# Attention logits: each head on its own 64 rows of the matmul array, instead of zero-padded keys on all 128

## The chip, the core and the metric

The kernel runs on one core of one Trainium2 chip. The metric is the device time of one execution in microseconds (us). The engines of the core run side by side, each with its own list of instructions in fixed order, and wait for one another through semaphores: PE (TensorE, matmuls), DVE (VectorE), ACT (ScalarE), POOL (GpSimd) and SP (the queue that issues DMAs). PE has two kinds of instruction, which the profile lists apart: a weight load (PEld), which puts the stationary operand into the array, and the matmul (PE), which streams the moving operand past it into a bank of PSUM. There are eight such banks here, each of 512 fp32 columns on 128 partitions.

## The reference

Two layers on x (1024 tokens, 1024 channels): dilated sliding-window attention, then a state-space layer. The change is in the attention, whose core is

```
DILATED_GROUPS = ((128, 1), (512, 4), (2048, 16))       # 3 groups, 16 heads of 64 channels
proj = h @ w_in                                         # q, k, v of each group, and a gate z
for g, (window, dilation):                              # token t looks at t - j*dilation, j = 0..window/dilation
    logits = einsum(q, k) * 64**-0.5 + rel_bias[bucket(distance)]
    lse = logsumexp(logits);  p = exp(logits - lse);  o = einsum(p, v)
o = sum over g of softmax_g(lse) * o_g
x = x + rms_norm((o * silu(z)) @ w_out)
...                                                     # layer 2: state-space, gelu, gated, projected
```

All arithmetic is fp32-like. The kernel gets this from fp32r matmuls by splitting each operand into a rounded part and a rest (`hi`, `lo`), and adding three products: hi*hi, hi*lo, lo*hi.

## The kernel before

The work runs in stages on one core: the values of all heads (0 to 372 us of the profiled execution), attention (372 to 1145 us), the output projection and norm of layer 1, then layer 2. In attention, `attn_pair` takes a pair of heads p = 0..7 (2 x 64 channels = 128 partitions), and in it the three groups g = 0, 1, 2. For each group it

- loads and splits the weights of q and k (`load_w`: DMA, ACT rounds to `whi`, POOL makes the rest `wlo`),
- projects (`proj_half`: 24 matmuls of 128x512 into a bank of the pool `psj`, twice for q, twice for k),
- brings the result from PSUM to SBUF, scaled, reordered and split (`evac_q`, `evac_k`: ACT writes hi, DVE writes lo),
- and calls `attn_unit` for u = 0, 1, four query tiles of 128 queries each: logits on PE into a bank of the pool `psl`, bias and maximum on DVE (line 488, one instruction per head and query tile, 128 or 256 keys wide), exponential on ACT, then transposes (`pt`, line 510) and the products with the values (`pso`, line 559 or 585).

Each of the four PSUM pools `psj`, `psl`, `pst`, `pso` has two banks.

How the two heads of a pair are kept apart in the logits: every matmul uses all 128 rows of the array, and a contraction has only 64 channels. For g = 0 and 1 the other 64 rows carry a second product. `qh` holds hi of head 0 on rows 0-63 and lo of head 0 on rows 64-127; `ql` holds the same of head 1, halves exchanged. `kh[:, h]` holds hi of head h on both halves (a second copy, line 214), and `kl[:, h]` holds lo of head h on one half and zeros on the other. So `q x kh` gives two of the three products and `q x kl` the third: two matmuls per head, four per query tile, 128 or 256 columns each. For g = 2 (128 keys per query tile) `qh` and `ql` hold both heads, and `kh[:, h]`, `kl[:, h]` have zeros on the rows of the other head, so that one matmul of 2 x 128 columns serves both heads: three per query tile. `zero_other` (POOL, line 221) writes those zeros into `kh` before each g = 2. There is one buffer of `kh` and one of `kl`, so the keys of a group are written only after the logits of the one before.

A scheduler sets the order on each engine, from the dependencies and its own estimate of times; work in `high_priority` (the weight loads and the evacuations of q and k) is pulled ahead. It mixes the logits of one group with the projections of the next, which is what the order below shows.

Of the kernel before, what the change touches and what calls it, by code (L numbers as in the profile page):

```python
# [23 lines left out]
P = 128  # L24
S = 1024
D = 1024
KT = 8
H = 512
# [8 lines left out]
ORD = (1, 4, 8)  # L37
# [3 lines left out]
def f32(ap):  # L41
    return ap.bitcast(F32)
# [3 lines left out]
HEADS = (slice(0, 64), slice(64, 128))  # L46
# [32 lines left out]
def split(c, hi, lo, src, scale=None, engine=None):  # L79

    nc = c.nc
    if scale is None:
        nc.scalar.copy(hi, src)  # L83
        return (engine or nc.vector).tensor_tensor(lo, src, f32(hi), op=ALU.subtract)  # L84
    else:
        nc.scalar.activation(hi, src, AF.Copy, scale=scale)
        nc.vector.scalar_tensor_tensor(lo, src, scale, f32(hi), op0=ALU.mult, op1=ALU.subtract)
# [101 lines left out]

def evac_q(c, ps, g, t0, q):  # L190


    nc = c.nc
    n = ps.shape[1] // ORD[g]
    at = (S - t0) // ORD[g] - n
    sv = ps.rearrange("p (l r) -> p r l", r=ORD[g])[:, :, ::-1]
    q = [t.rearrange("p (r l) -> p r l", r=ORD[g])[:, :, at:at + n] for t in q]
    a, b = HEADS
    for dh, dl, src in (((q[0], q[1], sv),) if g == 2 else ((q[0][a], q[0][b], sv[a]), (q[1][b], q[1][a], sv[b]))):
        nc.scalar.activation(dh, src, AF.Copy, scale=0.125)  # L200
        nc.vector.scalar_tensor_tensor(dl, src, 0.125, f32(dh), op0=ALU.mult, op1=ALU.subtract)


def evac_k(c, ps, g, t0, kh, kl):


    n = ps.shape[1] // ORD[g]
    at = t0 // ORD[g]
    sv = ps.rearrange("p (l r) -> p r l", r=ORD[g])
    for s in range(2):  # L210
        dh, dl = (t[:, s, :].rearrange("p (r l) -> p r l", r=ORD[g])[:, :, at:at + n] for t in (kh, kl))
        split(c, dh[HEADS[s]], dl[HEADS[s]], sv[HEADS[s]])
        if g < 2:
            c.nc.scalar.copy(dh[HEADS[1 - s]], sv[HEADS[s]])  # L214


def zero_other(c, t):

    for s in range(2):
        rows = HEADS[1 - s]  # L220
        c.nc.gpsimd.tensor_copy(t[rows, s, :], c.zt[rows].to_broadcast([64, S]))


def load_first(c, a, k):
# [35 lines left out]
class Quads:  # L260
# [45 lines left out]
    done, jobs = 0, {}  # L306
# [151 lines left out]
def ms_col(g, n, h, qt):  # L458

    return (n * 16 + h * 8 + 7 - qt, n * 16 + h * 8 + (qt ^ 1), n * 16 + h * 8 + qt)[g]  # L460


def attn_unit(c, g, u, q, k, v, bt, ms, O):


    nc = c.nc
    qh, ql = q
    kh, kl = k
    lg = c.attn.tile([P, 2, 4, 256], F32, tag="lg", name="lg", bufs=3)
    tiles = []  # L470
    for j in range(4):
        qt = u * 4 + j
        m = (7 - qt, 1 - qt % 2, 0)[g]
        start = (max(m - 1, 0) * P, qt // 2 * 256, qt * P)[g]
        w = 256 if m else 128
        tiles.append(w)
        ps = c.psl.tile([P, 2, 256], F32, tag="psl", name="psl")
        qs = slice(qt * P, qt * P + P)
        ks = slice(start, start + w)
        if g == 2:  # L480
            jobs = [(ps[:, :, 0:w], a, b[:, :, ks]) for a, b in ((qh, kh), (qh, kl), (ql, kh))]
        else:
            jobs = [(ps[:, h, 0:w], (qh, ql)[h], b[:, h, ks]) for h in range(2) for b in (kh, kl)]
        for n, (o, a, b) in enumerate(jobs):
            nc.tensor.matmul(o, a[:, qs], b, start=n == 0, stop=n == len(jobs) - 1, skip_group_check=True)  # L485
        for h in range(2):
            col = ms_col(g, 0, h, qt)
            nc.vector.tensor_tensor_reduce(  # L488
                lg[:, h, j, 0:w], ps[:, h, 0:w], bt[:, h, 256 - w:256], scale=1.0, scalar=-3.0e38,
                op0=ALU.add, op1=ALU.max, accum_out=ms[:, col:col + 1])  # L490
    nm = c.small.tile([P, 2, 4], F32, tag="nm", name="nm")
    at = (4 - 4 * u, 4 * u, 4 * u)[g]
    mx = ms[:, 0:16].rearrange("p (h t) -> p h t", h=2)[:, :, at:at + 4]
    nc.vector.tensor_scalar(nm, mx, -1.0, None, op0=ALU.mult)  # L494
    for h in range(2):
        for j, w in enumerate(tiles):
            col = ms_col(g, 1, h, u * 4 + j)
            b = (3 - j, j ^ 1, j)[g]
            nc.scalar.activation(lg[:, h, j, 0:w], lg[:, h, j, 0:w], AF.Exp, bias=nm[:, h, b:b + 1],  # L499
                                 accum_out=ms[:, col:col + 1])  # L500
    (pv_last if g == 2 else pv_first)(c, g, u, lg, v, O)
    if u == 1:
        put_ms(c, g, ms)
# [148 lines left out]
def attn_pair(c, p, w_in, h):  # L652
    nc = c.nc
    c.pair = p
    O = []
    for g in range(3):
        qh = c.attn.tile([P, S], F32R, tag="qh", name="qh", bufs=2)
        ql = c.attn.tile([P, S], F32R, tag="ql", name="ql", bufs=2)
        w = load_w(c, w_in[g * 8 + p])
        for th in range(2):  # L660
            src = proj_half(c, w, h[th])
            with c.tc.high_priority(AHEAD):
                evac_q(c, src, g, th * H, (qh, ql))
        bt = load_bias(c, p, g)
        if g == 2:
            zero_other(c, c.kh)
        w = load_w(c, w_in[(3 + g) * 8 + p])
        for th in range(2):
            src = proj_half(c, w, h[th])
            with c.tc.high_priority(AHEAD):  # L670
                evac_k(c, src, g, th * H, c.kh, c.kl)
        v = load_v(c, p, g)
        rotations(c, p, g)
        if g == 1:
            run_merge(c)
        ms = c.small.tile([P, 32], F32, tag="ms", name="ms")
        for u in range(2):
            attn_unit(c, g, u, (qh, ql), (c.kh, c.kl), v, bt, ms, O)
            if p and g == u == 0:
                merge_weights(c, p - 1)  # L680
    if p == 7:
        merge_weights(c, p)
    c.merge = lambda: merge(c, p, O)


def run_merge(c):
    if c.merge:
        c.merge()
    c.merge = None
# [20 lines left out]
def attention(c, a):  # L710
    nc, tc = c.nc, c.tc
    c.h = h = []
    c.w_engine = nc.vector
    c.merge = c.compact = None
    for th in range(2):
        hh = c.pa.tile([P, KT, H], F32R, tag=f"a{th}", name=f"hh{th}")
        hl = c.pa.tile([P, KT, H], F32R, tag=f"a{2 + th}", name=f"hl{th}")
        h.append((hh, hl))
    with tc.tile_pool(name="vphase", bufs=1, side="right", reuse_waits="tile") as pool:
        c.vslot = lambda n, dt: pool.tile([P, 4, H], dt, tag=f"v{n}", name=f"v{n}")  # L720
        c.vextra = pool.tile([P, 256], F32, tag="extra", name="extra")
# [12 lines left out]
        nc.sync.dma_start(gain, bass.AP(src.tensor, src.offset, [[0, P], [1, D]]))  # L734
        nc.vector.tensor_copy(c.identr, ident)

        def rows(i):
            if i + 1 < 8:
                load_x(i + 1)
            norm_transpose0(c, xs[i], sq, gain, h[i // 4], slice(i % 4 * P, i % 4 * P + P))  # L740

        v_phase(c, a, rows)

    c.attn = c.es_attn.enter_context(tc.tile_pool(name="attn", bufs=1, side="right", reuse_waits="tile"))
    c.kh = c.attn.tile([P, 2, S], F32R, tag="kh", name="kh")
    c.kl = c.attn.tile([P, 2, S], F32R, tag="kl", name="kl")
    zt = c.cst.tile([P, 1], F32, name="zt")
    nc.vector.memset(zt, 0.0)
    c.zt = zt
    zero_other(c, c.kl)  # L750
    c.w_engine = nc.gpsimd
    for p in range(8):
        attn_pair(c, p, a["w_in"], h)
    c.w_engine = nc.vector
    return h
# [861 lines left out]
```

## Time and profile before

| | |
|---|---|
| median of 3 runs | 1726.44 us (1725.02 to 1726.55) |
| the profiled execution | 1722.86 us, of which the span from the first to the last instruction is 1721.1 us |
| granted TensorE clock | 0.992 mean |
| PE busy | 1655.9 us (96%), 9262 matmuls |
| DVE, ACT, POOL busy | 1064.8, 799.9, 483.5 us |
| the logits matmuls (line 485) | 704 |

How to read it: a row of the timeline gives the start in us, the time taken, engine, line, operation, `out<-in`, and the form `rows*columns` of the stationary operand followed by the output. The ends of matmuls are modelled and overlap the next ones, so what one matmul costs PE is read from the distance between two starts, not from its duration. In a group of instructions, "idle before" is the idle time of that engine just before them, with what ended it.

### The profile page before, as it was taken

What the parts mean: (1) busy time and instruction counts of PE and PEld (TensorE: products, weight loads), DVE (VectorE), ACT (ScalarE), POOL (GpSimd) and SP (SyncE); (2) the same over time, 40 slices, a digit from 0 to 9 for tenths busy, and PEclk for the clock granted to TensorE, in tenths of its full rate; (3) what the DMA queues carried; (4) which work ended last, traced back from release to release, by engine and by line L of the source; (5) the groups of instructions that cost most, each with busy time, mean ns of one, the idle gap of its engine ahead of it and who ended that gap; (6) DMA issues with size and microseconds to landing.
All of it is one profiled execution on the core that took longest, in us unless ns stands there. A gap on an engine that the chain in (4) does not pass through costs nothing. (4 is left out here: it accounts for less than half of the span.)

```text
span 1721.1 us, 25792 instructions
## 1 busy us (share of the span) xinstructions
PE 1655.9 (96%) x9262; PEld 1415.1 (82%) x9262; DVE 1064.8 (62%) x2582; ACT 799.9 (46%) x1872; POOL 483.5 (28%) x321
## 2 busy tenths in 40 slices
PE   6999999999999999999999999988998999989998
PEld 5889999988888788888888888876886887867886
DVE  7698798735566556566555565557462777764533
ACT  5232222246656656656756756653442232243411
POOL 2000000041242432524342442405210344413121
PEclk9999999999999999999999999999999999999999
DMA  6223454441242323323232423327259766465432
GB/s 236 91 52 102 137 181 154 128 144 53 55 111 80 87 80 91 88 74 105 79 107 73 116 81 98 112 71 200 86 166 232 206 211 219 139 186 167 141 122 86
DMA packets 176900, 212.68 MB, mean 124 GB/s; under 512 B 37361, under 2 KB 133380, under 8 KB 176772
## 3 DMA queue, kind: packets, MB, share of 16 engines
q1 hardware_dynamic: 176772, 211.04, 40.9%
q8 instruction: 73, 1.20, 0.3%
q14 instruction: 55, 0.45, 0.1%
HBM read 154.03 MB, written 56.96 MB: 123 GB/s over the span
## 5 line engine op out<-in xcount | busy, mean ns | idle before, releaser
L110 PE MATMUL psj<-hh,whi 128*128 128x512 f32 x896 | 360.4, 402 | 16.2 <-ACT kh L214 8.5
L110 PE MATMUL psj<-hh,wlo 128*128 128x512 f32 x896 | 359.6, 402 | 0.3 <-POOL wlo L84 0.3
L110 PE MATMUL psj<-hl,whi 128*128 128x512 f32 x896 | 357.9, 399 | 0.0
L110 PEld LDWEIGHTS psj<-hh,whi 128*128 128x128 f32 x896 | 169.8, 189 | 51.6 <-ACT kh L214 10.6
L84 POOL TENSOR_TENSOR wlo<-wraw,whi 128x1024 fp32r<-128x1024 f32 x48 | 115.4, 2405 | 335.7 <-ACT whi L83 329.4
L110 PEld LDWEIGHTS psj<-hh,wlo 128*128 128x128 f32 x896 | 169.6, 189 | 35.8 <-POOL wlo L84 0.7
L110 PEld LDWEIGHTS psj<-hl,whi 128*128 128x128 f32 x896 | 169.8, 190 | 33.5
L499 ACT ACTIVATE lg<-lg,nm 128x128 f32<-128x128 f32 (+1 forms) x384 | 168.1, 440 | 18.9 <-DVE nm L494 18.0
L83 ACT CAST whi<-wraw 128x1024 fp32r<-128x1024 f32 x80 | 83.8, 1047 | 141.9 <-PE psj L110 97.4
L488 DVE CUSTOM_DVE_ANT_0 lg<-psl,T 128x128 f32<-128x128 f32 (+1 forms) x384 | 115.8, 346 | 53.5 <-PE psl L485 52.1
L84 DVE TENSOR_TENSOR ph<-pt,ph 128x512 fp32r<-128x512 f32 (+2 forms) x160 | 97.2, 621 | 37.4 <-ACT ph L83 35.3
L389 PE MATMUL psq<-whi,v 128*128 128x256 f32 x640 | 118.7, 283 | 0.0
L110 PE MATMUL psj<-h1h,whi 128*128 128x512 f32 (+1 forms) x272 | 107.0, 394 | 10.3 <-DVE z L1402 7.9
L84 DVE TENSOR_TENSOR kl<-psj,kh 64x512 fp32r<-64x512 f32 x96 | 66.0, 688 | 70.7 <-ACT kh L83 70.0
L570 DVE TENSOR_TENSOR O<-O,pso 64x512 f32<-64x512 f32 x64 | 44.2, 691 | 103.3 <-ACT O L569 102.6
L110 PE MATMUL psj<-h1l,whi 128*128 128x512 f32 (+1 forms) x272 | 105.4, 388 | 0.2 <-DVE h1l L84 0.2
L110 PE MATMUL psj<-h1h,wlo 128*128 128x512 f32 (+1 forms) x272 | 105.0, 387 | 0.0
L389 PEld LDWEIGHTS psq<-whi,v 128*128 128x128 f32 x640 | 99.5, 189 | 1.0 <-ACT whi L83 0.6
L83 ACT CAST ph<-pt 128x512 fp32r<-128x512 f32 (+2 forms) x160 | 81.6, 533 | 35.9 <-PE pt L510 34.7
L510 PE MATMUL pt<-identr,lg 128*128 128x128 f32 x560 | 93.5, 275 | 0.0
L559 PE MATMUL pso<-ph,vs 128*128 128x256 f32 (+1 forms) x544 | 89.9, 275 | 2.8 <-ACT ph L83 1.5
L559 PEld LDWEIGHTS pso<-ph,vs 128*128 128x128 f32 x544 | 81.6, 189 | 13.1 <-ACT ph L83 2.6
(287 smaller groups left out, 3862.7 us busy)
## 6 DMA issues: line engine op xcount, KB each, us to landing
wraw<-in_w_in_dram SPq DMA_DIRECT2D x56, 512.0 KB
mw<-wt_dr SPq DMA_DIRECT2D x48, 256.0 KB
v<-in_w_v_dram SPq DMA_DIRECT2D x20, 512.0 KB
vp<-v_dr SPq DMA_DIRECT2D x16, 512.0 KB
wraw<-in_ssm_w_in_dram SPq DMA_DIRECT2D x16, 512.0 KB
v_dr<-v SPq DMA_DIRECT2D x30, 256.0 KB
rot_dr<-rt SPq DMA_DIRECT2D x48, 128.0 KB
ca_dr<-ca SPq DMA_DIRECT2D x32, 144.0 KB
```

The costliest lines, as they stand in the source:

```text
L83: nc.scalar.copy(hi, src)
L84: return (engine or nc.vector).tensor_tensor(lo, src, f32(hi), op=ALU.subtract)
L110: nc.tensor.matmul(ps, a[:, s], b[:, k, :], start=first and k == 0 and n == 0, stop=k == KT - 1 and n == 2, skip_group_check=True)
L389: nc.tensor.matmul(o, r[x][:, k, ts], w[y][:, k, :], skip_group_check=True, start=i in (0, 4, 5) and t % 2 == k == n == 0, stop=k == 3 and ...
L488: nc.vector.tensor_tensor_reduce(lg[:, h, j, 0:w], ps[:, h, 0:w], bt[:, h, 256 - w:256], scale=1.0, scalar=-3.0e38, op0=ALU.add, op1=ALU.m ...
L499: nc.scalar.activation(lg[:, h, j, 0:w], lg[:, h, j, 0:w], AF.Exp, bias=nm[:, h, b:b + 1], accum_out=ms[:, col:col + 1])
L510: c.nc.tensor.transpose(pt[:, n * P:(n + 1) * P], lg[:, h, j, part * P:part * P + P], c.ident)
L559: nc.tensor.matmul(o, l, r, start=n == 0, stop=n == len(jobs) - 1, skip_group_check=True)
L570: nc.vector.tensor_tensor(dst, dst, fr[1], op=ALU.add)
```

## The change

Queries and keys are each split once, all 128 partitions in one instruction of ACT and one of DVE: `qh`, `ql`, `kh`, `kl` hold both heads, head 0 on partitions 0-63 and head 1 on 64-127. There is no second copy of the keys and there are no zeros, and `zero_other` goes. `kh` and `kl` get two buffers. The logits of a head are a matmul of 64 rows: rows 0-63 of the array for head 0, rows 64-127 for head 1, hi*hi, hi*lo, lo*hi for each, alternating between the heads: six matmuls per query tile in place of four or three. Two query tiles are taken together, and the two banks of `psl` are now one per head (each with both query tiles), where they were one per query tile (each with both heads). In the built program the logits are 1152 matmuls in place of 704, each with a tile of 64x128 of the array; nearly all the others have 128x128.

```diff
 def evac_q(c, ps, g, t0, q):
-    nc = c.nc
     n = ps.shape[1] // ORD[g]
     at = (S - t0) // ORD[g] - n
-    sv = ps.rearrange("p (l r) -> p r l", r=ORD[g])[:, :, ::-1]
-    q = [t.rearrange("p (r l) -> p r l", r=ORD[g])[:, :, at:at + n] for t in q]
-    a, b = HEADS
-    for dh, dl, src in (((q[0], q[1], sv),) if g == 2 else ((q[0][a], q[0][b], sv[a]), (q[1][b], q[1][a], sv[b]))):
-        nc.scalar.activation(dh, src, AF.Copy, scale=0.125)
-        nc.vector.scalar_tensor_tensor(dl, src, 0.125, f32(dh), op0=ALU.mult, op1=ALU.subtract)
+    hi, lo = (t.rearrange("p (r l) -> p r l", r=ORD[g])[:, :, at:at + n] for t in q)
+    split(c, hi, lo, ps.rearrange("p (l r) -> p r l", r=ORD[g])[:, :, ::-1], 0.125)

-def evac_k(c, ps, g, t0, kh, kl):
+def evac_k(c, ps, g, t0, k):
...
-    sv = ps.rearrange("p (l r) -> p r l", r=ORD[g])
-    for s in range(2):
-        dh, dl = (t[:, s, :].rearrange("p (r l) -> p r l", r=ORD[g])[:, :, at:at + n] for t in (kh, kl))
-        split(c, dh[HEADS[s]], dl[HEADS[s]], sv[HEADS[s]])
-        if g < 2:
-            c.nc.scalar.copy(dh[HEADS[1 - s]], sv[HEADS[s]])
+    hi, lo = (t.rearrange("p (r l) -> p r l", r=ORD[g])[:, :, at:at + n] for t in k)
+    split(c, hi, lo, ps.rearrange("p (l r) -> p r l", r=ORD[g]))

 def attn_unit(c, g, u, q, k, v, bt, ms, O):
-    for j in range(4):
...
-        ps = c.psl.tile([P, 2, 256], F32, tag="psl", name="psl")
...
-        if g == 2:
-            jobs = [(ps[:, :, 0:w], a, b[:, :, ks]) for a, b in ((qh, kh), (qh, kl), (ql, kh))]
-        else:
-            jobs = [(ps[:, h, 0:w], (qh, ql)[h], b[:, h, ks]) for h in range(2) for b in (kh, kl)]
-        for n, (o, a, b) in enumerate(jobs):
-            nc.tensor.matmul(o, a[:, qs], b, start=n == 0, stop=n == len(jobs) - 1, skip_group_check=True)
+    for j0 in (0, 2):
+        banks = [c.psl.tile([P, 2, 256], F32, tag="psl", name="psl") for _ in range(2)]
+        for j in (j0, j0 + 1):
...
+            for n, (x, y) in enumerate(((qh, kh), (qh, kl), (ql, kh))):
+                for ps, rows in zip(banks, HEADS):
+                    nc.tensor.matmul(ps[:, j - j0, 0:w], x[rows, qs], y[rows, ks],
+                                     start=j == j0 and n == 0, stop=n == 2, skip_group_check=True)
+        for j in (j0, j0 + 1):
...                                              # line 488's instruction, from banks[h][:, j - j0, 0:w]

 def attn_pair(c, p, w_in, h):
-        if g == 2:
-            zero_other(c, c.kh)
+        kh = c.attn.tile([P, S], F32R, tag="kh", name="kh", bufs=2)
+        kl = c.attn.tile([P, S], F32R, tag="kl", name="kl", bufs=2)
```

What it moves on PE, at two places. The first is head pair 0, group 0, the third and fourth query tile, between the projections of group 1 (`psj`). Before (names with their buffer numbers; each `psl` number is one bank, of one query tile):

```order
L110 MATMUL psj_4077<-hh1_111,wlo_4045 128x512
L485 MATMUL psl_3858<-kh_3684,qh_3690 128x256
L485 MATMUL psl_3858<-kl_3685,qh_3690 128x256
L485 MATMUL psl_3858<-kh_3684,ql_3691 128x256
L485 MATMUL psl_3858<-kl_3685,ql_3691 128x256
L485 MATMUL psl_3865<-kh_3684,qh_3690 128x256
L485 MATMUL psl_3865<-kl_3685,qh_3690 128x256
L485 MATMUL psl_3865<-kh_3684,ql_3691 128x256
L485 MATMUL psl_3865<-kl_3685,ql_3691 128x256
L110 MATMUL psj_4114<-hh0_109,whi_4110 128x512
```

After, the same two query tiles (bank 3846 is head 0, bank 3847 head 1):

```order
L466 MATMUL psl_3846<-kh_3748,qh_3684 128x256
L466 MATMUL psl_3846<-kl_3749,qh_3684 128x256
L466 MATMUL psl_3846<-kh_3748,ql_3685 128x256
L466 MATMUL psl_3847<-kh_3748,qh_3684 128x256
L466 MATMUL psl_3847<-kl_3749,qh_3684 128x256
L466 MATMUL psl_3847<-kh_3748,ql_3685 128x256
L466 MATMUL psl_3846<-kh_3748,qh_3684 128x256
L466 MATMUL psl_3847<-kh_3748,qh_3684 128x256
L466 MATMUL psl_3846<-kl_3749,qh_3684 128x256
L466 MATMUL psl_3847<-kl_3749,qh_3684 128x256
L466 MATMUL psl_3846<-kh_3748,ql_3685 128x256
L466 MATMUL psl_3847<-kh_3748,ql_3685 128x256
```

Eight matmuls of all 128 rows have become twelve of 64 rows, and they do not always alternate between the heads: here three of head 0 stand first and then three of head 1, because the scheduler expects head 0's bank to come free earlier.

The second place is head pair 1, group 1, where the transposes of group 0 (`pt`) fall due at the same time. Before:

```order
L510 MATMUL pt<-identr,lg 128x128 x7
L485 MATMUL psl<-kh,qh 128x256
L485 MATMUL psl<-kl,qh 128x256
L485 MATMUL psl<-kh,qh 128x128
L485 MATMUL psl<-kl,qh 128x128
L485 MATMUL psl<-kh,ql 128x128
L485 MATMUL psl<-kl,ql 128x128
L485 MATMUL psl<-kh,ql 128x256
L485 MATMUL psl<-kl,ql 128x256
L110 MATMUL psj<-hh_111,whi 128x512
```

After:

```order
L466 MATMUL psl<-kh,qh 128x256
L494 MATMUL pt<-identr,lg 128x128
L466 MATMUL psl<-kh,qh 128x256
L466 MATMUL psl<-kl,qh 128x256
L494 MATMUL pt<-identr,lg 128x128 x2
L466 MATMUL psl<-kl,qh 128x256
L466 MATMUL psl<-kh,ql 128x256
L494 MATMUL pt<-identr,lg 128x128 x4
L466 MATMUL psl<-kh,ql 128x256
L466 MATMUL psl<-kh,qh 128x128 x2
L466 MATMUL psl<-kl,qh 128x128 x2
L466 MATMUL psl<-kh,ql 128x128 x2
```

Transposes of 128x128 now stand between single logits matmuls of 64 rows. Over the whole program the 1152 matmuls stand in 240 unbroken runs (a transpose or any other matmul of 128 rows ends a run), of which 134 have three matmuls or fewer and 26 have all twelve; 97 runs are followed by a transpose, 143 by another matmul, and 138 end in a matmul of 128 columns.

The evacuation of q and k of pair 0, group 0 on ACT, before:

```order
L200 ACTIVATE qh<-psj 64x512
L200 ACTIVATE ql<-psj 64x512
L83 CAST kh<-psj 64x512
L214 CAST kh<-psj 64x512
L83 CAST kh<-psj 64x512
L214 CAST kh<-psj 64x512
L83 CAST whi<-wraw 128x1024
```

After:

```order
L86 ACTIVATE qh<-psj 128x512
L83 CAST kh<-psj 128x512
L83 CAST whi<-wraw 128x1024
L83 CAST kh<-psj 128x512
L86 ACTIVATE qh<-psj 128x4x128
```

One instruction for q and one for k of each half of the tokens, where two and four stood.

More of the change, by code (lines that the diff above doesn't have):

```diff
@@ L470, in attn_unit @@
     tiles = []
-    for j in range(4):
[L472 to L476, printed above, removed]
-        ps = c.psl.tile([P, 2, 256], F32, tag="psl", name="psl")
-        qs = slice(qt * P, qt * P + P)
-        ks = slice(start, start + w)
-        if g == 2:
-            jobs = [(ps[:, :, 0:w], a, b[:, :, ks]) for a, b in ((qh, kh), (qh, kl), (ql, kh))]
-        else:
-            jobs = [(ps[:, h, 0:w], (qh, ql)[h], b[:, h, ks]) for h in range(2) for b in (kh, kl)]
-        for n, (o, a, b) in enumerate(jobs):
[L485 to L490, printed above, removed]
+    for j0 in (0, 2):
+        banks = [c.psl.tile([P, 2, 256], F32, tag="psl", name="psl") for _ in range(2)]
+        for j in (j0, j0 + 1):
+            qt = u * 4 + j
+            m = (7 - qt, 1 - qt % 2, 0)[g]
+            start = (max(m - 1, 0) * P, qt // 2 * 256, qt * P)[g]
+            w = 256 if m else 128
+            tiles.append(w)
+            qs = slice(qt * P, qt * P + P)
+            ks = slice(start, start + w)
+            for n, (x, y) in enumerate(((qh, kh), (qh, kl), (ql, kh))):
[3 more added lines that the diff above has]
+        for j in (j0, j0 + 1):
+            w = tiles[j]
+            for h in range(2):
+                col = ms_col(g, 0, h, u * 4 + j)
+                nc.vector.tensor_tensor_reduce(
+                    lg[:, h, j, 0:w], banks[h][:, j - j0, 0:w], bt[:, h, 256 - w:256], scale=1.0, scalar=-3.0e38,
+                    op0=ALU.add, op1=ALU.max, accum_out=ms[:, col:col + 1])
     nm = c.small.tile([P, 2, 4], F32, tag="nm", name="nm")
@@ L670, in attn_pair @@
             with c.tc.high_priority(AHEAD):
-                evac_k(c, src, g, th * H, c.kh, c.kl)
+                evac_k(c, src, g, th * H, (kh, kl))
         v = load_v(c, p, g)
@@ L677, in attn_pair @@
         for u in range(2):
-            attn_unit(c, g, u, (qh, ql), (c.kh, c.kl), v, bt, ms, O)
+            attn_unit(c, g, u, (qh, ql), (kh, kl), v, bt, ms, O)
             if p and g == u == 0:
@@ L744, in attention @@
     c.attn = c.es_attn.enter_context(tc.tile_pool(name="attn", bufs=1, side="right", reuse_waits="tile"))
[L745 to L750, printed above, removed]
     c.w_engine = nc.gpsimd
```

4 lines of the change are left out of this document (removed).

## The prediction

> **What bounds the kernel now.** I read the busy shares of the page first, then the attention stage by itself, then the waits of PE.
>
> ```profile
> PE 1655.9 (96%) x9262; PEld 1415.1 (82%) x9262; DVE 1064.8 (62%) x2582; ACT 799.9 (46%) x1872; POOL 483.5 (28%) x321
> 372.00:1145.00 773.00, 761.69 (x4268) 652.33 (x4267) 444.79 (x1319) 495.75 (x1339) 277.58 (x153) 1.00 0.31 87
> PE psj L110 <- ACT kh L214: 8.5, 4, 2.6
> ```
>
> The second row is the stretch 372 to 1145 us, all of the attention: PE busy 761.69 of 773 us, DVE 444.79, ACT 495.75, POOL 277.58, and the granted clock 1.00. The third is what PE waits for there: four times, 8.5 us in all, for the second copy of the keys on ACT, which holds a `psj` bank. PE is the bound, and every nanosecond that the logits add to or take from its stream shows in the end time, up to these 8.5 us. So the question is what the 704 old and the 1152 new matmuls take of PE.
>
> ```profile
> L485 PE MATMUL psl<-kh,qh x192: 218/280/368, 372.9 to 1141.6; 128*128 128x256 f32 x152, 128*128 128x128 f32 x40
> L485 PE MATMUL psl<-kl,qh x192: 273/280/368, 373.0 to 1141.7; 128*128 128x256 f32 x152, 128*128 128x128 f32 x40
> L485 PE MATMUL psl<-kh,ql x192: 221/281/367, 373.4 to 1141.8; 128*128 128x256 f32 x152, 128*128 128x128 f32 x40
> L485 PE MATMUL psl<-kl,ql x128: 273/281/367, 373.5 to 1111.4; 128*128 128x256 f32 x88, 128*128 128x128 f32 x40
> ```
>
> ```profile
> 715.15 0.28 PE L485 MATMUL psl<-kh,qh 128*128 128x256 f32 x1
> 715.27 0.28 PE L485 MATMUL psl<-kl,qh 128*128 128x256 f32 x1
> 715.39 0.28 PE L485 MATMUL psl<-kh,ql 128*128 128x256 f32 x1
> 715.51 0.28 PE L485 MATMUL psl<-kl,ql 128*128 128x256 f32 x1
> 715.63 0.22 PE L485 MATMUL psl<-kh,qh 128*128 128x128 f32 x1
> 715.69 0.28 PE L485 MATMUL psl<-kl,qh 128*128 128x128 f32 x1
> 715.80 0.27 PE L485 MATMUL psl<-kh,ql 128*128 128x128 f32 x1
> 715.91 0.28 PE L485 MATMUL psl<-kl,ql 128*128 128x128 f32 x1
> 716.03 0.45 PE L110 MATMUL psj<-hh,wlo 128*128 128x512 f32 x1
> ```
>
> From start to start a matmul of 256 columns costs 0.12 us, one of 128 columns 0.11 us: hardly less for half the columns, because a new set of 128 weights stands before each and takes that long. There are 544 of the first (152 + 152 + 152 + 88) and 160 of the second: 544 x 0.12 + 160 x 0.11 = 83 us of PE for all logits.
>
> **The new matmuls.** Per head pair 11 query tiles have 256 keys and 13 have 128 (eight of these in group 2, where one matmul of 2 x 128 columns served both heads). Times six matmuls and eight pairs: 528 of 256 columns and 624 of 128, by the same prices 63 + 69 = 132 us, if a matmul of 64 rows takes PE as long as one of 128 and they follow one another: 49 us more than before. If the two heads' matmuls, which use different rows, different weights and different banks, run side by side, each adjoining pair costs one price. Were all 576 pairs adjoining, that is 66 us, 17 less than before. In the program's order they aren't: where three of head 0 stand before three of head 1, or a transpose stands between, partners are parted. Counting run by run, with a matmul beside its neighbour only where the neighbour is the other head's, I get 80 us: 3 less than before. No row of this trace shows two matmuls side by side, so the two ends are -3 and +49. I take -3, since nothing that the two share is visible (other rows, other banks), but not with much confidence: each still loads 128 columns of weights, and one load is what 0.11 us is.
>
> **The change of array shape.** Nearly all matmuls have a tile of 128x128; the new ones have 64x128, in 240 runs, so PE changes shape 480 times. The trace has a few narrower matmuls, and they show what that costs.
>
> ```profile
> 155.39 0.28 PE L389 MATMUL psq<-wlo,v 128*128 128x256 f32 x1
> 155.51 0.28 PE L389 MATMUL psq<-whi,v 128*128 128x256 f32 x1
> 155.72 0.81 PE L175 MATMUL psb<-oneh,relx 33*16 33x384 f32 x2
> 156.46 0.39 PE L389 MATMUL psq<-whi,hh 128*128 128x256 f32 x1
> 156.69 0.27 PE L389 MATMUL psq<-wlo,hh 128*128 128x256 f32 x1
> 156.80 0.28 PE L389 MATMUL psq<-whi,hl 128*128 128x256 f32 x1
> ...
> 242.30 0.39 PE L389 MATMUL psq<-whi,v 128*128 128x256 f32 x2
> 242.62 0.41 PE L1214 MATMUL pk<-ca,O 128*32 128x128 f32 x2
> 242.95 0.33 PE L1226 MATMUL ptb<-identr,zr 128*128 128x128 f32 x1
> 243.04 0.36 PE L389 MATMUL psq<-wlo,v 128*128 128x256 f32 x1
> ...
> 1338.33 0.39 PE L110 MATMUL psj<-h1h,wlo 128*128 128x512 f32 x1
> 1338.56 0.94 PE L1344 MATMUL pv<-U,BT 128*128 128x128 f32 x7
> ```
>
> On the way in, the last wide matmul is followed after 0.21 us in place of 0.12 (155.51 to 155.72): 0.09 us lost. On the way out, the second of the two `pk` starts 0.13 after the first (0.41 less the 0.28 that one takes), at 242.75, and the transpose 0.20 after that in place of 0.11: 0.09 us again. And the first wide matmul outside keeps PE 0.23 us (156.46 to 156.69) where its kind keeps it 0.12: 0.11 us more, the length of a load of 128 columns, which elsewhere lies under the matmul before. A transpose outside keeps it 0.09 (242.95 to 243.04) where others keep it 0.03 (one stands at 617.32 below): 0.06 more. The last two rows are the control: matmuls of the same full fp32 type with a tile of 128x128 follow the wide ones at once (0.23), so it is the shape and not the type that costs.
>
> For the new runs: on the way in 0.09, and the first weights, here 128 columns, lie bare too: 0.11 (the `pk` of 32 columns lost 0.02 there: 0.13 against 0.11). On the way out 0.09, and 0.06 ahead of a transpose (97 runs) or 0.11 ahead of another (143). Sum: 240 x (0.20 + 0.09) + 97 x 0.06 + 143 x 0.11 = 70 + 6 + 16 = 91 us; less 0.05 for the 138 runs that end in 128 columns, whose 0.11 already holds a weight load that the way out counts again: 84 us. All of it is on PE, which nothing covers. Its ends: no row has a tile of 64x128. The nearest, 33*16, is narrower in rows and columns; the `pk` in columns alone. If only a change in columns costs, the term is 0; if the shape costs but the weights are loaded meanwhile, it is 240 x 0.18 = 43. I take 84, for both kinds of row agree to a hundredth whether rows are cut or not.
>
> The Trainium skill says in "TensorEngine Tiling (Array Packing)", section Key Properties, that changing the tiling mode drains the TensorE, and that a change of tile within a mode doesn't; by it the term is 84 and not 0. The rows with 33*16 and 128*32 agree (0.09 each way); that a mode of 64x128 does it too no run shown so far tells.
>
> One row speaks against a price for every narrow matmul:
>
> ```profile
> 616.97 0.51 PE L559 MATMUL pso<-ph,vs 128*128 128x256 f32 x3
> 617.32 0.27 PE L597 MATMUL ptm<-identr,ms 128*32 128x128 f32 x1
> 617.35 0.54 PE L559 MATMUL pso<-ph,vs 128*128 128x256 f32 x3
> ```
>
> This transpose into 32 columns is entered and left without a loss (616.97 + 3 x 0.12 = 617.33). A transpose may be run in the full shape whatever its width; the new logits aren't transposes.
>
> **What is taken off the other engines.**
>
> ```profile
> L83 ACT CAST kh<-psj 64x512 fp32r<-64x512 f32 x96 | 55.8, 582 | 32.6 <-PE psl L485 17.0 <-DVE kl L84 12.2 <-PE psj L110 2.4
> L214 ACT CAST kh<-psj 64x512 fp32r<-64x512 f32 x64 | 37.1, 580 | 34.6 <-DVE kl L84 34.1
> L200 ACT ACTIVATE qh<-psj 128x512 fp32r<-128x512 f32 x16 | 9.5, 592 | 2.6 <-PE psj L110 2.2
> L84 DVE TENSOR_TENSOR kl<-psj,kh 64x512 fp32r<-64x512 f32 x96 | 66.0, 688 | 70.7 <-ACT kh L83 70.0
> L221 POOL CAST kh<-zt 64x1024 fp32r<-64x1024 f32 x16 | 16.6, 1039 | 63.0 <-PE psl L485 62.5
> L488 DVE CUSTOM_DVE_ANT_0 lg<-psl,T 128x256 f32<-128x256 f32 x176 | 66.6, 419 | 42.0 <-PE psl L485 41.0
> ```
>
> An instruction on 128 partitions takes as long as one on 64 (592 against 580 ns). So ACT loses 112 instructions for k and 32 for q at 0.58 us, 84 us; DVE 48 and 32 at 0.69, 55 us; POOL the zeros, 18 x 1.04 = 19 us, and its 62.5 us of waiting for the old logits, behind which the `wlo` of the next weights stand in POOL's list. A `psj` bank is freed after one step of ACT and one of DVE, not after up to four and two, and the second key buffer takes away the 17.0 us that ACT waits for old logits. All of this lies beside a busy PE; of it only PE's own wait for the second copy shows, 8.5 us. That goes: -8. SP loses nothing.
>
> What it adds: both `psl` banks of a step are held until DVE has read two query tiles, four instructions of 0.42 us and a little more between them, some 2 us; the next step's matmuls wait behind them. In the order 23 matmuls of 128x512 mostly stand between, 23 x 0.23 = 5.3 us, which covers it; behind a logits matmul that waited nevertheless the whole PE list would stand. Where only two or three short matmuls stand between, up to 1 us could be lost, a few times per pair: 0 to 8 us. I take 0.
>
> **Sum.** -3 (logits) + 84 (shape) - 8 (PE's wait) = +73 us. The profiled execution was 1722.86 us with a span of 1721.1; the median of the runs is 1726.44, 3.6 above it. On the median: 1799 us.
>
> **The rivals.**
> (a) The shape of 64x128 costs nothing, and the heads run side by side: -3 - 8 = -11, 1715 us, faster. For it: the transpose above, and that no row has this very shape. Against it: the rows with 33*16. It decides from where a change in and out costs less than 11/240 = 0.05 us; the rows say 0.28 to 0.40. For this rival a page can be named: the Trainium skill, "TensorE: Matmul & The Clock Gate", Part 3, tells of four row tiles that ran 3.07 times as fast as one after the other, and that loads overlap where the row groups differ. No row here shows it.
> (b) The shape costs, and the two heads' weights or matmuls follow one another: +49 + 84 - 8 = +125, 1851 us. For it: 0.11 us per matmul is a weight load even now.
> (c) The shape costs half, with the loads hidden: -3 + 43 - 8 = +32, 1758 us.
> (d) No price for the shape, but one after the other: +49 - 8 = +41, 1767 us.
>
> **Chances.** My forecast 0.41, (a) 0.17, (b) 0.22, (c) 0.12, (d) 0.08. A change of 0.2% (3.5 us) is about what a measurement of this kernel tells from none. Only (a) ends faster: 0.17; a small price that just eats the gain leaves 0.03 for no change; slower 0.80. The range leaves out (a) alone: from just under (c), 1755, to just over (b), 1853.
>
> **What would show it.** In the timeline after, the first logits matmul of a run should follow its forerunner 0.09 us late, and the first wide matmul behind a run should keep PE 0.23 or more in place of 0.12 (0.34 for 512 columns); within a run the two heads' matmuls should start nearly together and each such pair keep PE 0.11 to 0.12 us; PE's wait for the copies should be gone, ACT at some 716 us busy and DVE at 1010. PE would stay busy through the attention, which grows by the 73 us, and the stages behind it should keep their lengths. I am wrong if the starts in and out of a run are as close as among wide matmuls (a), or if the starts within a run are 0.11 apart (b).

## The result, and the profile after

| | before | after |
|---|---|---|
| median | 1726.49 us (1725.02 to 1727.56, 4 runs) | 1771.44 us (1769.35 to 1776.26, 4 runs) |
| the profiled execution | 1722.86 us, span 1721.1 | 1776.26 us, span 1774.5 |
| from the first to the last logits matmul | 769.0 us | 826.4 us |

The changed kernel is slower: ratio 1.0265, 95% interval 1.0242 to 1.0288, or 45 us between the medians. The profiled executions are 53.4 us apart, since the one after lies 4.8 above its median and the one before 3.6 below. All of it stands in the attention. These are the stretches before and behind the last logits matmul (columns: us, then busy us of PE, PEld, DVE, ACT and POOL, granted clock, DMA share, GB/s), first of before, then of after:

```profile
372.88:1141.85 768.97, 757.66 (x4251) 649.06 (x4250) 442.74 (x1309) 494.29 (x1333) 276.70 (x153) 1.00 0.31 87
1141.85:1721.10 579.25, 541.01 (x2569) 442.74 (x2567) 334.98 (x661) 188.49 (x367) 169.77 (x134) 0.98 0.54 163
```

```profile
369.33:1195.69 826.36, 826.36 (x4697) 658.15 (x4696) 393.06 (x1234) 414.53 (x1197) 259.33 (x136) 1.00 0.28 80
1195.69:1774.50 578.81, 541.53 (x2572) 448.04 (x2570) 327.61 (x660) 187.79 (x366) 167.58 (x134) 0.97 0.54 164
```

The attention begins 3.6 us earlier and takes 57.4 us more, at the same granted clock of 1.00; what follows has its old length. PE is now busy in every one of the 826.36 us, where it had 11 us of idle time; ACT and DVE have 80 and 50 us less to do. So what the other engines lost bought only PE's idle time, and PE's own work grew by 69 us.

From the page of after, the busy shares and the groups that answer to those shown of before (busy us, mean ns of one, idle us of the engine ahead of them and what ended it):

```profile
PE 1721.2 (97%) x9710; PEld 1425.0 (80%) x9710; DVE 1004.7 (57%) x2501; ACT 714.5 (40%) x1728; POOL 460.8 (26%) x303
...
L110 PE MATMUL psj<-hh,whi 128*128 128x512 f32 x896 | 361.6, 404 | 6.1 <-DVE tz L779 6.1
```

ACT 714.5 and DVE 1004.7 us are what was forecast (716 and 1010). The projections into `psj` no longer wait for the second copy of the keys (16.2 us of idle time before, 8.5 of it for that copy).

The first logits of attention in PE's timeline after (`x2` are two instructions that the view joins; two of the six pairs are left out):

```profile
369.00 0.40 PE L110 MATMUL psj<-hh,wlo 128*128 128x512 f32 x1
369.33 0.39 PE L466 MATMUL psl<-kh,qh 64*128 64x256 f32 x2
369.55 0.28 PE L466 MATMUL psl<-kl,qh 64*128 64x256 f32 x2
369.67 0.27 PE L466 MATMUL psl<-kh,ql 64*128 64x256 f32 x2
...
370.02 0.28 PE L466 MATMUL psl<-kh,ql 64*128 64x256 f32 x2
370.23 0.50 PE L110 MATMUL psj<-hh,whi 128*128 128x512 f32 x1
370.56 0.39 PE L110 MATMUL psj<-hl,whi 128*128 128x512 f32 x1
```

Twelve matmuls are six pairs, each pair 0.12 us from the next: the two heads run side by side. Around them stands the price of the shape. On the way in, 0.33 us pass from 369.00 to 369.33 where a wide matmul keeps PE 0.23. The first pair keeps PE 0.22 us where the others keep it 0.12, since no weight load lies under the matmul before. On the way out it is 0.21 (370.02 to 370.23) in place of 0.12, and the first wide matmul keeps PE 0.33 in place of 0.23, for the same reason as the first pair. That is 0.39 us for this run. It is paid again for every run, however short:

```profile
382.68 0.29 PE L466 MATMUL psl<-kh,qh 64*128 64x256 f32 x2
382.90 0.33 PE L494 MATMUL pt<-identr,lg 128*128 128x128 f32 x1
383.16 0.39 PE L466 MATMUL psl<-kl,qh 64*128 64x256 f32 x2
383.48 0.98 PE L494 MATMUL pt<-identr,lg 128*128 128x128 f32 x7
384.39 0.39 PE L466 MATMUL psl<-kh,ql 64*128 64x256 f32 x2
384.71 0.50 PE L110 MATMUL psj<-hl,whi 128*128 128x512 f32 x1
```

A single pair between transposes (383.16, 384.39) keeps PE 0.32 us instead of 0.12, and delays what stands on both sides besides. The weight loads show the same. A wide matmul's load stands one matmul ahead (that of 369.00 starts at 368.77); the load of the first pair starts only with its matmul, at 369.33. Over the program the loads of the logits have 33.8 us of idle time ahead of them, with nothing that they wait for:

```profile
368.77 0.19 PEld L110 LDWEIGHTS psj<-hh,wlo 128*128 128x128 f32 x1
369.33 0.19 PEld L466 LDWEIGHTS psl<-kh,qh 64*128 64x128 f32 x2 [0.37 <-issue]
```

```profile
PEld psl L466 <- issue: 33.8, 145, 0.4
```

**PE's time for the logits.** To compare kernels I take the stretch from the matmul ahead of the first logits matmul to the end of the last, and charge every other matmul its usual distance to the next start (0.232 us for 512 columns, 0.118 for 256, 0.110 for 128). What is left is PE's stalls far from any logits, and the logits with all that they delay around them:

| | runs of logits | PE for the logits, us | stalls, us |
|---|---|---|---|
| before | 166 | 84.4 | 15.2 |
| after | 240 | 156.8 | 0.8 |

The 84.4 of before agree with the 83 of the prediction's prices. After the change the logits take 72.5 us more, and 14.4 us of stalls are gone: +58.

### The profile page after: what moved, and what is told of

It reads as the page before. It is cut to its first block, busy times and chain, and to the rows that moved or that the text cites. A ratio compares the mean times of both kernels' runs of the same rounds, so it can differ in the third digit from the quotient of the medians.

```text
span 1774.5 us, 26321 instructions
## 1 busy us (share of the span) xinstructions
PE 1721.2 (97%) x9710; PEld 1425.0 (80%) x9710; DVE 1004.7 (57%) x2501; ACT 714.5 (40%) x1728; POOL 460.8 (26%) x303
## 5 line engine op out<-in xcount | busy, mean ns | idle before, releaser
L494 PE MATMUL pt<-identr,lg 128*128 128x128 f32 x560 | 105.9, 284 | 0.0
L543 PE MATMUL pso<-ph,vs 128*128 128x256 f32 (+1 forms) x544 | 94.8, 277 | 0.0
L371 PE MATMUL psq<-wlo,v 128*128 128x256 f32 x320 | 89.8, 281 | 1.7 <-DVE wlo L84 1.7
```

The lines of the kernel that those rows point to most:

```text
L371: nc.tensor.matmul(o, r[x][:, k, ts], w[y][:, k, :], skip_group_check=True, start=i in (0, 4, 5) and t % 2 == k == n == 0, stop=k == 3 and ...
L494: c.nc.tensor.transpose(pt[:, n * P:(n + 1) * P], lg[:, h, j, part * P:part * P + P], c.ident)
L543: nc.tensor.matmul(o, l, r, start=n == 0, stop=n == len(jobs) - 1, skip_group_check=True)
```

## Experiments

Each was timed beside the kernel before on the same chip. The stretches quoted run from the first to the last logits matmul.

**The shape taken away, the order kept** (`e1_all_rows`, against the changed kernel). The matmuls run over both heads' rows, so the logits of the two heads are not kept apart.

```diff
-                    nc.tensor.matmul(ps[:, j - j0, 0:w], x[rows, qs], y[rows, ks],
+                    nc.tensor.matmul(ps[:, j - j0, 0:w], x[:, qs], y[:, ks],
```

> The changed kernel with each logits matmul over all 128 rows instead of the head's own 64 (so both heads' products are added up and the logits are not those of one head): the same 1152 matmuls in the same order, without a change of array shape and without two side by side. My theory (a change into and out of 64 rows costs about 0.32 us of PE, 240 times, 77 us, and the heads do run side by side, which saves 52 us against one after the other): 77 go, 52 come, so 25 less than the changed kernel, about 1746 us (1738 to 1756). Rival 1, the slowdown lies in having 448 more matmuls and not in the shape: as the changed kernel or above, 1771 to 1823. Rival 2, it lies in holding both banks for two query tiles and in the order that follows: no change, 1771.

1745.13 us (1743.36 to 1750.38, 5 runs), ratio to before 1.0104 (1.0088 to 1.0120). The same transposes and logits as above, in the same order:

```profile
368.07:1168.37 800.30, 800.30 (x4696) 698.43 (x4695) 384.63 (x1234) 415.03 (x1197) 259.89 (x136) 1.00 0.30 83
```

```profile
382.57 0.27 PE L494 MATMUL pt<-identr,lg 128*128 128x128 f32 x1
382.60 0.49 PE L466 MATMUL psl<-kl,qh 128*128 128x256 f32 x2
382.92 0.93 PE L494 MATMUL pt<-identr,lg 128*128 128x128 f32 x7
```

From the lone transpose to the next ones PE needs 0.35 us, where it needed 0.58 in the 64-row shape (382.90 to 383.48), although the two logits matmuls now run one after the other. PE's time for the logits is 131.2 us, against 132 by prices for 1152 matmuls one after another at no price for the runs. So the 240 runs cost nothing in themselves; the shape is what makes them cost.

**Fewer, unbroken runs** (`e2_unbroken`, against the changed kernel): the twelve matmuls of a step are chained in PE's list, so that nothing is put between, and the heads alternate.

```diff
+        with c.tc.high_priority(AHEAD):
+            last = None
+            for o, x, y, first, stop in jobs:              # the same matmuls, as a list
+                with (c.tc.issue_after(last.ins) if last else ExitStack()):
+                    mm = nc.tensor.matmul(o, x, y, start=first, stop=stop, skip_group_check=True)
...                                                         # the first waits for DVE's last read of both banks
```

> The changed kernel with the twelve matmuls of a step kept together: they have priority on PE, each is queued behind the one before, and the first waits until DVE has read both banks. 118 runs in place of 240, and all 576 pairs adjoin. My theory: 122 runs fewer at 0.32 us are 39 us, and adjoining pairs make 66 us of logits in place of 80, 14 more: 53 less than the changed kernel, about 1719 us (1710 to 1732), which would be near or a little below the kernel before. Rival 1 and 2 (more matmuls; both banks held): nothing of that changes, about 1771.

1720.93 us (1717.15 to 1726.37, 6 runs), ratio 0.9958 (0.9941 to 0.9975). 118 runs in place of 240 (not 96, one for each step: in 22 steps the first pair still stands apart from the other ten matmuls):

```profile
367.54:1143.53 775.99, 775.99 (x4695) 632.52 (x4695) 396.91 (x1233) 409.81 (x1196) 263.55 (x136) 1.00 0.31 86
```

Attention is 50.4 us shorter than after, and PE's time for the logits 106.6 us: 50.2 less, 8.4 of it because all partners now adjoin (74.4 and 66.0 in the table below) and the other 42 for 122 runs fewer. With the same matmuls in the same shape, what decides is above all how often PE goes in and out. Attention is still 7.0 us longer than in the kernel before. That the whole is a little faster comes from the stretches around it: in the profiled executions attention begins 5.3 us earlier, and what stands behind it is 7.4 us shorter; no run explains these.

**Fewer still** (`e8_fewer_runs`, against the unbroken version).

```diff
+    steps = ((0, 1, 2, 3),) if g == 2 else ((0, 1), (2, 3))
+    for js in steps:
-    for j0 in (0, 2):
...
-            for n, (x, y) in enumerate(((qh, kh), (qh, kl), (ql, kh))):
+            for n, (x, y) in enumerate(((qh, kl), (ql, kh), (qh, kh))):
```

> The unbroken version (118 runs, pairs adjoining) with the four query tiles of group 2 in one step, and the products in the order hi*lo, lo*hi, hi*hi: 80 runs of logits in place of 118, with the same 1152 matmuls. Theory (each run costs PE 0.34 us for the change of array shape and back): 38 x 0.34 = 13 us less than the unbroken version, 1708 us (1702 to 1715). Rival (the cost goes with the matmuls, or the longer steps hold the two banks of psl so long that PE waits): 1718 to 1728.

1701.58 us (1699.79 to 1704.30, 5 runs), ratio 0.9840 (0.9827 to 0.9854): a little below the expected range, and the fastest of all kernels run.

```profile
369.08:1122.54 753.46, 753.46 (x4656) 628.40 (x4656) 385.56 (x1219) 407.68 (x1190) 256.62 (x134) 1.00 0.31 88
```

PE's time for the logits is 91.9 us, 14.7 less than with 118 runs, or 0.39 for each run saved; the two edits, longer steps in group 2 and another order of the products, are not told apart. The other 8 of the 22 us by which attention is shorter are no gain: they are matmuls that now stand behind the last logits, where they still have to be run. Against before, the logits are still 7.5 us dearer (91.9 and 84.4), and some 15 us of stalls are gone: 7 us less of PE. The profiled executions are 18.6 us apart. Of the rest, 3.8 us are an earlier start, and some 8 us come from the stretch behind the last logits, which holds 8 us more of matmuls and took only 0.7 us longer; no run shows why. The kernel before with nothing but its stalls taken away took 1710 us (below), 9 more than this one, and its logits cost what they cost before. So it isn't shown that the shape itself gains anything, even in 80 runs.

**The heads apart** (`e3_heads_apart`, against the changed kernel).

```diff
-            for n, (x, y) in enumerate(((qh, kh), (qh, kl), (ql, kh))):
-                for ps, rows in zip(banks, HEADS):
+            for ps, rows in zip(banks, HEADS):
+                for n, (x, y) in enumerate(((qh, kh), (qh, kl), (ql, kh))):
```

> The changed kernel with the three matmuls of head 0 ahead of the three of head 1 in each query tile, where they alternated. 242 runs, as many as before it (240), but only a last and a first matmul of the two heads meet, so the logits take 109 us in place of 80 if meeting is what lets two run side by side. My theory: 30 more than the changed kernel, about 1801 us (1790 to 1810). If running side by side gave nothing, or did not need them to alternate: 1771.

1800.55 us (1792.35 to 1801.85, 5 runs), ratio 1.0407 (1.0387 to 1.0427). The time was as expected, but the trace gives another reason than I had:

```profile
368.67:1220.62 851.95, 851.95 (x4706) 680.19 (x4705) 388.44 (x1238) 415.30 (x1198) 259.29 (x136) 1.00 0.28 78
```

Where three matmuls of head 0 and then three of head 1 stood together, they still ran in pairs (0.49 us for such a run of 128 columns, where three of one head alone take 0.48). What cost was that the scheduler now parted whole groups: 73 of the 242 runs hold three or more of one head alone, where none of the 240 did. PE's time for the logits grew by 23.6 us, where the rule that a matmul starts no earlier than its forerunner in the list gives 30. That led to the next two runs.

**How far apart partners may stand** (`e10_three_by_three` and `e11_head_by_head`, against the version of 80 runs): A A A B B B within a query tile, and all of A, then all of B, within a step.

```diff
-            for n, (x, y) in enumerate(((qh, kl), (ql, kh), (qh, kh))):
-                for ps, rows in list(zip(banks, HEADS)):
+            for ps, rows in list(zip(banks, HEADS)):                   # e10_three_by_three
+                for n, (x, y) in enumerate(((qh, kl), (ql, kh), (qh, kh))):
...
+        jobs = jobs[0::2] + jobs[1::2]                                 # e11_head_by_head, the loops as they were
```

> The version of 80 runs with one edit: within a query tile the three matmuls of head 0 stand first, then the three of head 1, where they alternated; the same 1152 matmuls in the same 80 unbroken runs. Theory (PE lets the matmuls of one half of the rows run ahead of those of the other half that stand before them in its list, so that partners need not stand beside one another): no change, 1702 us (1697 to 1707), and 66 us of PE inside the runs as before. Rival (the prediction's rule, by which a matmul starts no earlier than the one before it in the list): 97 us in place of 66, so 1733 us (1726 to 1738).

> The version of 80 runs with one edit: all matmuls of head 0 of a step first (six; twelve in group 2), then all of head 1. Theory (the two halves of the rows run as independent streams, however far apart partners stand): 1702 us (1697 to 1707). Rival 1 (in the order of the list): 123 us in place of 66, so 1759 us (1750 to 1765). Rival 2 (PE looks ahead only by some few instructions; the kernel with the heads apart showed partners up to five apart): the runs of 12 stay, and the 16 runs of 12 + 12 lose up to 16 x 0.11 x 6 = 11 us, 1713 us.

Three by three: 1707.40 us (1704.17 to 1711.35, 6 runs), ratio 0.9885 (0.9865 to 0.9906). Its attention, and its first run, whose twelve stand in PE's list as `kl,qh`, `kh,ql`, `kh,qh` of head 0, the same three of head 1, and so again:

```profile
368.97:1119.44 750.47, 750.47 (x4637) 626.05 (x4637) 394.85 (x1217) 406.23 (x1187) 257.23 (x134) 1.00 0.32 88
```

```profile
368.97 0.39 PE L473 MATMUL psl<-kl,qh 64*128 64x256 f32 x2
369.19 0.29 PE L473 MATMUL psl<-kh,ql 64*128 64x256 f32 x2
369.31 0.28 PE L473 MATMUL psl<-kh,qh 64*128 64x256 f32 x2
...
369.87 0.50 PE L110 MATMUL psj<-hh,whi 128*128 128x512 f32 x1
```

The pairs form all the same: head 1's `kl,qh` starts with head 0's, ahead of two matmuls that stand before it in the list. Inside the runs (from the first logits matmul of each to the next other matmul) PE needs 79.4 us against 79.0 with the heads alternating. (The median is 5.8 us above that of the version of 80 runs, just outside what was expected. Attention itself is 3.0 us shorter in the trace, and the stretch behind the last logits matmul is 10 us longer. 3.7 us of this are 19 matmuls that the scheduler put behind instead; the other 6 lie in stages that the edit doesn't touch.)

Head by head: 1739.77 us (1738.37 to 1745.93, 6 runs), ratio 1.0074 (1.0053 to 1.0094). Six of head 0, then six of head 1:

```profile
369.17 0.38 PE L474 MATMUL psl<-kl,qh 64*128 64x256 f32 x1
369.39 0.28 PE L474 MATMUL psl<-kh,ql 64*128 64x256 f32 x1
369.51 0.28 PE L474 MATMUL psl<-kh,qh 64*128 64x256 f32 x1
369.51 0.39 PE L474 MATMUL psl<-kl,qh 64*128 64x256 f32 x2
369.74 0.28 PE L474 MATMUL psl<-kh,ql 64*128 64x256 f32 x2
369.85 0.28 PE L474 MATMUL psl<-kh,qh 64*128 64x256 f32 x2
...
370.21 0.28 PE L474 MATMUL psl<-kh,qh 64*128 64x256 f32 x1
370.42 0.51 PE L110 MATMUL psj<-hh,whi 128*128 128x512 f32 x1
```

Head 1's first (the long one of the two joined at 369.51) starts with head 0's third, four places ahead of it in the list, and three of the six of each head run beside the other's. Inside the runs PE needs 116.1 us, 37 more than with the heads alternating; in the order of the list it would be 57 more, as two free streams none. So the second rival had the mechanism, a look-ahead of a few instructions, but I had put its reach at more than six: it is four matmuls here.

**The stall of the kernel before** (`e7_copy_sbuf` and `e5_copy_pool`, both against before): the second copy of the keys read from the first copy instead of the `psj` bank, by ACT as before, or by POOL.

```diff
-            c.nc.scalar.copy(dh[HEADS[1 - s]], sv[HEADS[s]])
+            c.nc.scalar.copy(dh[HEADS[1 - s]], dh[HEADS[s]])               # e7_copy_sbuf
+            c.nc.gpsimd.tensor_copy(dh[HEADS[1 - s]], dh[HEADS[s]])        # e5_copy_pool
```

> The kernel before with one edit: the second copy of the keys is still made by ACT, but is read from the first copy in SBUF and not from the bank psj, so that the bank is free after one step of ACT and one of DVE on each head's half, and the copy doesn't stand behind DVE's reading of the bank. Theory (PE's stalls in attention, 15 us in the kernel before, come from psj banks held too long, and nothing else waits on the copy): the stalls go, 1712 us (1708 to 1720). Rival (a freed bank only moves the wait to the next buffer, as it did when POOL made the copy): 1723 to 1730 or more, with PE waiting elsewhere for as long.

> The kernel before, with one thing taken off the chain that holds a projection's bank: the second copy of the keys for groups 0 and 1 is made by POOL from the first copy in SBUF, not by ACT from PSUM. My theory, that the changed kernel wins back 8 to 14 us of PE's waits because the bank comes free sooner: about 8 of them come back here, 1718 us (1713 to 1723). Rival: those waits came from the one key buffer and not from the bank, or they only move: 1726, or more if the key is late because POOL is.

By ACT: 1710.43 us (1709.48 to 1711.12, 4 runs), ratio 0.9893 (0.9880 to 0.9907), as expected. PE's waits in attention fall from 11.3 us to 1.5, and none is for the copy any more. ACT's timeline at one of the three long ones (2.7 us of PE each), first before:

```profile
591.25 0.58 ACT L83 CAST kh<-psj 64x512 fp32r<-64x512 f32 x1
591.86 0.51 ACT L499 ACTIVATE lg<-lg,nm 128x256 f32<-128x256 f32 x1
...
595.93 0.58 ACT L214 CAST kh<-psj 64x512 fp32r<-64x512 f32 x1
```

and with the copy read from SBUF:

```profile
593.08 0.58 ACT L83 CAST kh<-psj 64x512 fp32r<-64x512 f32 x1
593.69 0.62 ACT L214 CAST kh<-kh 64x512 fp32r<-64x512 f32 x1
```

The old copy had been put behind seven of the eight exponentials of an attention unit, 4.7 us behind the split of the same half, and held the bank all that time. So the wait that the trace named, ACT's copy, was long because of what stood ahead of the copy in ACT's list. The edit takes away both the late place and the reading of the bank; which of the two would have been enough isn't shown.

By POOL: 1758.56 us (1753.74 to 1759.04, 4 runs), ratio 1.0168 (1.0154 to 1.0183), a miss by 40 us. The copy's wait went and another came:

```profile
PE pso L559 <- DVE ph L84: 21.6, 22, 1.8
```

```profile
598.86 0.68 DVE L84 TENSOR_TENSOR kl<-psj,kh 64x512 fp32r<-64x512 f32 x1
599.46 1.42 DVE L494 TENSOR_SCALAR nm<-ms 128x8 f32<-128x8 f32 x1
600.79 0.67 DVE L84 TENSOR_TENSOR kl<-psj,kh 64x512 fp32r<-64x512 f32 x1
601.39 0.67 DVE L84 TENSOR_TENSOR ph<-pt,ph 128x512 fp32r<-128x512 f32 x1
```

The split of the keys now stands in DVE's list ahead of that of the probabilities, for which PE waits. One such place is shown; why a reduction of eight columns took 1.42 us there, and how the 40 us divide, stays open.

**One key buffer** (`e9_one_key_buffer`, against the changed kernel): `bufs=2` taken from `kh` and `kl`.

> The changed kernel with one buffer of kh and of kl in place of two; all else alike, 250 runs of logits in place of 240. Theory (the single split alone frees the bank early enough, and the second buffer covers nothing that PE waits for): 10 more runs x 0.33 = 3 us, 1775 us (1770 to 1780). Rival (the second buffer is what took PE's stalls away): some 10 to 15 us more than the changed kernel, 1781 to 1787, with PE waiting for the split of the keys.

1781.28 us (1778.96 to 1782.71, 4 runs), ratio 1.0302 (1.0288 to 1.0316), 6 us more than the changed kernel by the ratios. The time doesn't decide: the median lies at the lower end of the rival's range, the 6 us within the theory's. The trace speaks for the theory:

```profile
L83 ACT CAST kh<-psj 128x512 fp32r<-128x512 f32 x48 | 28.0, 583 | 16.7 <-PE psl L466 14.3 <-PE psj L110 2.4
...
L466 PE MATMUL psl<-kh,qh 64*128 64x128 f32 (+1 forms) x384 | 72.3, 316 | 0.9 <-ACT kh L83 0.9
```

ACT waits for the old logits again, 14.3 us, but PE for the keys only 0.9. PE's time for the logits is 163.1 us, 6.3 more, with 250 runs for 240 (3.4 at 0.34). So the single split freed PE, not the second buffer; 3 us of the 6.3 stay open.

## Why the prediction came out

The forecast, 1799 us, had the right side and the main mechanism, the price of the shape, and was 28 us too high: +73 on the median where it was +45. The rivals (d), 1767, and (c), 1758, came nearer to 1771 than the forecast did; the time alone couldn't have told them apart, and the traces do. By its own terms:

**Shape: +84, held.** With pairs counted as they really ran, the 64-row kernels give nearly the same price per run, 0.32 to 0.35 us (head by head is left out, since its partners ran neither together nor apart):

| | runs | logits alone, heads as two streams | PE for the logits | price of a run |
|---|---|---|---|---|
| after | 240 | 74.4 | 156.8 | 0.343 us |
| one key buffer | 250 | 75.0 | 163.1 | 0.352 |
| heads apart | 242 | 95.5 | 180.4 | 0.351 |
| unbroken | 118 | 66.0 | 106.6 | 0.344 |
| 80 runs | 80 | 66.0 | 91.9 | 0.324 |
| three by three | 80 | 66.0 | 93.5 | 0.344 |

(The second column is, run by run, the longer of the two heads' sums at 0.12 and 0.11 us.) For the changed kernel 240 x 0.343 = 82 us, against 84. The parts were 0.09 on the way in and on the way out, 0.06 ahead of a transpose, 0.11 ahead of another matmul. Two parts were off, and they nearly cancel. The first weights lie bare for 0.11 ahead of 256 columns, as taken, but for 0.05 ahead of 128, with which 99 runs begin: 6 us too much. And the 0.05 taken off for the 138 runs that end in 128 columns wasn't there: such a last matmul keeps PE 0.20 us, 0.09 over its 0.11, so 7 us were lacking. That the sum came so near is in part luck; still, the few rows of 33*16 and 128*32 had foretold each way in and out of the 64-row shape to a hundredth.

**Logits: -3, too small a gain; it was -10.** This is the step that failed in its reason. That partners are parted "where three of head 0 stand before three of head 1" does not hold: PE starts a matmul of the other head ahead of up to three that stand before it. Two streams give 74.4 us, not 80, and before had 84.4.

**PE's wait: -8, too small; it was -14.** I took what the list of waits showed for the second copy, 8.5 us. From start to start the four waits cost 9.1 us (three of 2.7 and one of 0.9), and some 4 us more were waits for ACT's and DVE's split of the probabilities, which I had left standing; 2 us more are delays too small to be named. In the changed kernel nearly all of it is gone; with the copy read from SBUF most of it goes without any change of shape (1710 us).

Together -10 + 82 - 14 = +58, and 57.4 were measured. The attention began 3.6 us earlier, which I had not looked for and which no run explains, and the last stages were 0.4 shorter: +53.4 between the profiled executions. The other 8 us to the medians are where those two executions stand among their runs.

**What cost nothing, as said.** Two `psl` banks held for two query tiles: no logits matmul waited in the changed kernel. DVE and ACT: beside a busy PE.

**The rivals.** (a), no price, needed 0.05 us a run: it is 0.34. (b) and (d) needed the heads one after the other: they start together. (d) is in effect the kernel over all rows: its logits cost 131.2 us, as (d) has it, and its 1745 us lie below (d)'s 1767 by the larger stalls that are gone and by shorter stretches around attention. (c), half the price, would have left 43 us where 82 were paid.

## What to carry to other kernels

Before matmuls are moved to a part of the array, count how many unbroken runs PE's list will hold, not how many matmuls: here one run costs 0.34 us, as much as three matmuls of 256 columns, so twelve matmuls in six paired steps (0.70 us and 0.34) still lose against eight over all rows (0.96), and a run broken by transposes loses several times over. Even in 80 runs the logits stayed 7.5 us dearer than in the kernel before. Chain such matmuls in the list, make the runs long, and let DVE's read be the only thing that the first waits for. And where a wait names an instruction, look at what that instruction stood behind on its own engine: one operand changed (`sv` to `dh`) gave 1% without any of the rest.

## What the runs showed of the hardware

- Where they alternate, two matmuls on the two halves of the rows start within 15 ns of one another (all 576 pairs of the version of 80 runs), and a pair takes as long as one alone, weight loads included: 0.12 us for 256 columns, 0.11 for 128.
- PE doesn't keep the order of its list between the two halves. With three and three it ran them as pairs; with six and six, head 1's first started with head 0's third. The Trainium skill, "TensorE: Matmul & The Clock Gate", Part 3, The mechanism, says that matmuls start and end strictly in the order of the program; here they did not.
- Going from 128x128 to 64x128 and back costs 0.09 us each way, and the first weights after each change lie bare (0.05 to 0.11 us). The Trainium skill, "TensorEngine Tiling (Array Packing)", Key Properties, says that a change of mode drains the engine and that tiles run independently: both agree with these rows. Transposes into 32 columns (128*32) between 128x128 matmuls cost nothing.
- The stretch behind the last logits matmul took from 572 us (unbroken) to 590 us (three by three) in single executions of kernels with the same code there. The 58 matmuls more that the scheduler put there in the second, some 12 us at their usual distances, are two thirds of it; the other 6 us stay open. So a difference of 5 us between two medians, even with narrow intervals, was not enough to judge an edit in attention by; its own stretch of the trace was.
